# One list of steps for the late stages of a hybrid residual block: gates and latent projection with tokens stationary, merge turned by transposes

## The chip, the cores and the metric

The kernel runs on one core of one Trainium2 chip. The time is the device time of one execution in microseconds (us). TensorE (PE in the profile) multiplies, VectorE (DVE), ScalarE (ACT) and GpSimd (POOL) work element by element, and SyncE (SP) only issues DMAs. Each engine takes its own instructions in order; between engines, semaphores say when a tile is ready or free. TensorE multiplies a stationary tile of 128 x 128, loaded first, with a moving tile of up to 512 columns; N is the number of moving columns. Products add up in banks of the accumulator memory of 128 x 512 numbers, of which the kernel has eight, four called `acc` and four called `aux`.

## What is computed

The input has 512 tokens of 2048 channels. One normalised copy `h` feeds three branches, a gate for each, and one output projection:

```python
h = rms_norm(x, norm_g[l])
proj = h @ w_in[l]
(c_gate, b_gate, u, conv_z, c_q, c_kv, k_rope_raw, mla_z,
 mem_q, mem_z, g_conv, g_mla, g_mem) = jnp.split(proj, split_at, axis=-1)
conv_y = b_gate * causal_depthwise_conv(c_gate * u, conv_w[l])
o_conv = (conv_y * jax.nn.silu(conv_z)) @ w_conv_out[l]
...
o_mla = (mla_y * jax.nn.silu(mla_z)) @ w_mla_out[l]
...
o_mem = (mem_y * jax.nn.silu(mem_z)) @ w_mem_out[l]
merged = (jax.nn.sigmoid(g_conv) * o_conv + jax.nn.sigmoid(g_mla) * o_mla
          + jax.nn.sigmoid(g_mem) * o_mem)
x = x + merged @ w_o[l]
```

`mla_y` is latent attention with 16 heads over the 512 tokens, `mem_y` is attention of 4 heads of width 256 into 256 memory tokens. `g_conv`, `g_mla`, `g_mem`, `o_*` and `merged` are 512 x 2048; `w_mla_out` and `w_o` are 2048 x 2048, `w_mem_out` and `w_conv_out` 1024 x 2048.

## The kernel before

**Products.** Every matrix is kept as two parts, hi and lo, whose sum is the number in fp32. `split` (L121) makes them: ACT copies to hi (L122), DVE subtracts to lo (L124); `weights` (L137) does the same for a weight chunk (L146, L147). One product of two such matrices is three matmuls, `mm3` (L150): hi by hi (L153), hi by lo (L154), lo by hi (L155). A weight chunk is one DMA of 512 KB, 128 partitions x 1024 numbers.

**Two layouts.** A dense product can have the weights stationary and the tokens moving (mode "F", the result has channels on the partitions), or the tokens stationary and the weights moving (mode "T", the result has tokens on the partitions). Both move N = 512 columns.

**Seven products for eight.** The large late projections are cut into 2 x 2 blocks of channels and tokens and use seven block products, P1 to P7, in place of eight. Sums of blocks of the weights are made by DVE as they come (L893 in `s_weights`, L1028 in `t_run`), sums of blocks of the tokens once ahead (`form_sums` L834, in `Forms.build` and `build_forms`). `s_group` (L906) keeps the weights stationary: a block of tokens is then 256 wide, so its matmuls move N = 256, and 512 output columns take 336 of them. `t_run` (L997) keeps the tokens stationary: the weights move with N = 512, and 1024 output columns take 336 matmuls. Before, only `w_o` uses `t_run`.

**Stages.** The memory's keys and values, the latents, the 16 heads, then two groups of memory queries (`mem_queries` L737) with two heads of memory attention each (`mem_attend` L752), then the late stages:

1. `memz`: a dense product in mode "F" over 16 chunks in two groups (L1095 to L1113); its result, through SiLU, multiplies the memory attention's output, which has gone through memory (`mydram`). Meanwhile DVE and ACT make the block sums of `h` (`build_forms`, `place_t1`).
2. 24 `s_group`s in one `s_run` (L966): eight for the convolution branch, four for `mla_z`, twelve for the gates (four each for `g_mem`, `g_conv`, `g_mla`), whose sigmoid is stored to memory (`gdram`) with channels on the partitions.
3. `mem_out`: `branch` (L1172), a dense product in mode "F"; each result times its gate goes to `mdram`. Beside it the block sums for the next stage are made.
4. `mla_out`: four `s_group`s; each result times its gate, plus `mdram`, goes back to `mdram`.
5. `conv_out`: `branch` again; the result times its gate plus `mdram` is the merged row, with channels on the partitions as `w_o` needs it, and `conv_result` makes its block sums.
6. `w_o`: two groups of `t_run`, plus x, to the output.

**Order.** Each stage opens pools of buffers of its own and closes them at its end; a buffer of the next stage lies where one of the last lay, and its first writer waits for the last reader there. The compiler's scheduler sets the order on all engines but SP, whose queue keeps the order of the program. That one queue carries the weight chunks and, between them, the loads of `araw`, `e`, `o`, `sg`, `gm`, `m` and `x` (activations, gates, partial merges, input). `t_run` loads weights eight chunks ahead; `s_group` loads its eight chunks at its first step; `branch` loads its activations at its first four steps.

Of the kernel before, what the change touches and what calls it, by code (L numbers as in the profile page):

```python
# [43 lines left out]
BUILD = (0, 2, 3, 5, 6, 8, 9, 12)  # L44
# [50 lines left out]
def body(ctx, tc, a, out):  # L95
# [11 lines left out]
    wpool = Lines(ctx.enter_context(tc.tile_pool(name="wts", bufs=2)), small, "wts")  # L107
    small.tile([P, SMALL_FILL], F32, name="fill")
    top = ctx.enter_context(tc.tile_pool(name="top", bufs=1, side="right"))
    top.tile([P, TOP_FILL], F32, name="topfill")  # L110
    dram = ctx.enter_context(tc.tile_pool(name="dram", bufs=1, space=bass.MemoryType.DRAM))
# [693 lines left out]
    for _ in mem_query_steps(1, banks_m):  # L805
# [6 lines left out]

    adram = dram.tile([32, P, S], F32, name="adram")
    gdram = dram.tile([48, P, S], F32, name="gdram")
    mdram = dram.tile([KB, P, S], F32, name="mdram")
    PRODUCTS = (("P1", "X", "00"), ("P7", "Y", "T3"), ("P5", "Z", "T1"), ("P6", "W", "T2"),
                ("P2", "X", "10"), ("P4", "Y", "T4"), ("P3", "Z", "11"))

    def tokens_of(b0, b1, f):

        return {"00": (b0[:, 0, :HS], b0[:, 1, :HS]), "T1": (b0[:, 0, HS:], b0[:, 1, HS:]),  # L830
                "10": (b1[:, 0, :HS], b1[:, 1, :HS]), "11": (b1[:, 0, HS:], b1[:, 1, HS:]),
                "T3": (f[:, 0, 0], f[:, 1, 0]), "T2": (f[:, 0, 1], f[:, 1, 1]), "T4": (f[:, 0, 2], f[:, 1, 2])}

    def form_sums(e, o, t, t1):  # L834
        vec.tensor_tensor(out=t[:, 0], in0=o[:, HS:], in1=e[:, HS:], op=ALU.subtract)
        vec.tensor_tensor(out=t[:, 1], in0=t[:, 0], in1=e[:, :HS], op=ALU.add)
        vec.tensor_tensor(out=t[:, 2], in0=o[:, :HS], in1=t[:, 1], op=ALU.subtract)
        vec.tensor_tensor(out=t1, in0=e[:, HS:], in1=e[:, :HS], op=ALU.subtract)

    class Forms:  # L840


        def __init__(self, name):
            self.p, self.close = open_pool(name, "right")
            mk = lambda n, w: [self.p.tile([P, 2] + w, F32R, name=f"{n}{p}") for p in range(8)]
            self.b0, self.f, self.b1 = mk("b0", [S]), mk("f", [3, HS]), mk("b1", [S])
            self.B = [tokens_of(*t) for t in zip(self.b0, self.b1, self.f)]

        def build(self, p, e, o, pool_, first=False):

            b0, b1, f = self.b0[p], self.b1[p], self.f[p]
            t = pool_.tile([P, 3, HS], F32, tag="t", name="t", bufs=2)
            form_sums(e, o, t, e[:, HS:])
            split(e, b0[:, 0], b0[:, 1])
            split(t, f[:, 0], f[:, 1])
            split(o, b1[:, 0], b1[:, 1])

    def open_weights():

        nonlocal psw, close_sw  # L860
        psw, close_sw = open_pool("swts", "left")
        psw.tile([P, KC, 512], F32, tag="raw", name="raw", bufs=6)
        sraw[0] = sform[0] = 0

    psw = close_sw = None
    sraw, sform, sbank = [0], [0], [0]

    def load_s(src):
        i = sraw[0]
        sraw[0] = (i + 1) % 10  # L870
        p = wpool if i % 5 < 2 else psw
        t = p.tile([P, KC, 512], F32, tag="raw", name="raw", bufs=4 if p is wpool else 6)
        t = t.rearrange("p k n -> p (k n)")
        nc.sync.dma_start(t, src)
        return t

    def s_weights(name, w, ch):

        w00, w01, w11, w10 = (w[2 * i + ch] for i in range(4))
        if name == "P1":  # L880
            src = w00
        elif name == "P2":
            src = w10
        elif name == "P4":
            src = w11
        elif name == "P7":
            src = psw.tile([P, KC, 512], F32, tag="s3", name="s3", bufs=2).rearrange("p k n -> p (k n)")
            vec.tensor_tensor(out=src, in0=w00, in1=w01, op=ALU.subtract)
        else:
            src = w01  # L890
            i0, i1, op = {"P5": (w01, w11, ALU.add), "P6": (w01, w00, ALU.subtract),
                          "P3": (w10, w01, ALU.subtract)}[name]
            vec.tensor_tensor(out=src, in0=i0, in1=i1, op=op)  # L893
        i = sform[0]
        sform[0] = (i + 1) % 3
        p = wpool if i < 2 else psw
        hi = p.tile([P, KC, 512], F32R, tag="whi", name="whi", bufs=2 if p is wpool else 1)
        lo = p.tile([P, KC, 512], F32R, tag="wlo", name="wlo", bufs=2 if p is wpool else 1)
        hi, lo = (t.rearrange("p k n -> p (k n)") for t in (hi, lo))
        split(src, hi, lo)  # L900
        return tuple(t.rearrange("p (k n) -> p k n", k=4) for t in (hi, lo))

    def pair(t):
        return t.rearrange("p (b t) -> p b t", b=2)

    def s_group(src, consume, B, pr, add=None):  # L906

        sbank[0] += 1  # L910
        tag = "acc" if sbank[0] % 2 else "aux"
        w, bk, sc = [], {}, {}
# [39 lines left out]
        for name, bn, xn in PRODUCTS:  # L952
            def products(ws, name=name, bn=bn, xn=xn):
                first = bn not in bk
                if first:
                    bk[bn] = bank(tag)
# [459 lines left out]
```

## Time and profile before

| | |
|---|---|
| time, median of 3 runs | 2211.53 us (2210.7 to 2213.6) |
| the profiled execution | 2212.02 us |
| its span, first to last instruction | 2209.8 us, mean granted TensorE clock 0.994 |
| busy: PE, DVE, ACT, POOL | 2151.9, 1604.6, 1026.5, 159.5 us |
| memory moved by DMA | 317.87 MB |
| memory attention, second half, with `memz` | 614 to 721 us |
| 24 `s_group`s | 721 to 1689 us |
| `mem_out` | 1693 to 1782 us |
| `mla_out` | 1782 to 1947 us |
| `conv_out` | 1954 to 2042 us |
| `w_o` | 2044 to 2205 us |

The stages run one after the other on TensorE, so the difference of two starts is a stage's time. The spans and waits below are read from the one profiled execution. In a row of a timeline the columns are the start, the duration, the engine, the line, the operation, what it writes and reads, how many such rows are taken together, and in brackets the idle time just before with what ended it. In a table of windows they are the window, its length, then for PE, weight loads, DVE, ACT and POOL the busy time and number of instructions, then the granted clock, the share of the DMA engines and GB/s.

### The profile page before, as it was taken

To read this page: it belongs to the slowest core of one execution; us is meant where nothing else is said; L and a number is where in the kernel's file an instruction comes from. 1 tells how busy PE (TensorE), PEld (TensorE's weight loads), DVE (VectorE), ACT (ScalarE), POOL (GpSimd) and SP (SyncE) were. 2 spreads that over 40 slices of the span, in tenths; PEclk is the share of its full clock that TensorE was granted. 3 is DMA by queue.
4 is the path that set the end of the run, shared out by engine and by line. 5 is a ranking of instruction groups with operands and counts; after the bars stand their busy time and mean duration, and the time that the engine had idled before them with its cause. 6 is when DMAs were issued, how large, how long until landed. Compare 5 with 4: busy or idle time off the path is not lost.

```text
span 2209.8 us, 35712 instructions
## 1 busy us (share of the span) xinstructions
PE 2151.9 (97%) x14456; PEld 1991.8 (90%) x14456; DVE 1604.6 (73%) x2195; ACT 1026.5 (46%) x1547; POOL 159.5 (7%) x147
## 2 busy tenths in 40 slices
PE   7999999999999999999999999999999999989999
PEld 5788889888887999999999999999998899978787
DVE  7853777774448887887887777767766778867887
ACT  5532677764334444444444444444444434433443
POOL 7510311120000000000000000000000000000000
PEclk9999999999999999999999999999999999999999
DMA  7573212244234433323444344343334755366463
GB/s 260 161 254 105 81 63 68 67 148 148 86 100 160 152 114 119 106 91 130 139 151 164 125 134 141 122 150 115 115 134 151 260 199 189 136 207 231 162 200 115
DMA packets 109845, 317.87 MB, mean 144 GB/s; under 512 B 12144, under 2 KB 12400, under 8 KB 109680
## 3 DMA queue, kind: packets, MB, share of 16 engines
q1 hardware_dynamic: 85296, 269.10, 37.1%
q10 hardware_dynamic: 22784, 41.25, 5.0%
q0 software_dynamic: 1600, 5.24, 0.7%
q8 instruction: 113, 1.85, 0.3%
q14 instruction: 52, 0.43, 0.1%
HBM read 267.31 MB, written 48.23 MB: 143 GB/s over the span
## 4 chain that ended last, share of the span: by engine, by line
PE 89%; DVE 4%; ACT 2%; issue 1%; DMA 1%; POOL 1%; SPq 0%; ACTq 0%; DVEq 0%; POOLq 0%
PE acc L153 16%; PE acc L154 16%; PE acc L155 16%; PE aux L154 12%; PE aux L153 12%; PE aux L155 12%; DVE wlo L147 1%; PE aux L204 1%; PE aux L660 1%; DVE wlo L124 1%; ACT whi L146 1%; POOL xs L304 1%; DVE hT L126 0%; PE aux L640 0%; PE aux L641 0%
## 5 line engine op out<-in xcount | busy, mean ns | idle before, releaser
L122 ACT ACTIVATE whi<-raw 128x1024 fp32r<-128x1024 f32 x392 | 415.3, 1060 | 626.3 <-PE acc L154 236.1
L124 DVE TENSOR_TENSOR wlo<-raw,whi 128x1024 fp32r<-128x1024 f32 x392 | 477.6, 1222 | 162.3 <-ACT whi L122 161.9
L147 DVE TENSOR_TENSOR wlo<-raw,whi 128x1024 fp32r<-128x1024 f32 (+3 forms) x153 | 187.6, 1227 | 173.0 <-ACT whi L146 170.7
L146 ACT ACTIVATE whi<-raw 128x1024 fp32r<-128x1024 f32 (+3 forms) x153 | 152.0, 993 | 218.1 <-PE acc L155 78.5
L893 DVE TENSOR_TENSOR raw<-raw 128x1024 f32<-128x1024 f32 x168 | 205.4, 1223 | 25.6 <-DMA raw<-in_w_conv 7.6
L153 PE MATMUL acc<-f,whi 128*128 128x256 f32 x672 | 190.3, 283 | 1.6 <-ACT whi L122 1.6
L155 PE MATMUL acc<-f,wlo 128*128 128x256 f32 x672 | 190.3, 283 | 0.8 <-DVE wlo L124 0.8
L153 PE MATMUL aux<-f,whi 128*128 128x256 f32 x672 | 190.2, 283 | 0.0
L154 PE MATMUL aux<-f,whi 128*128 128x256 f32 x672 | 190.2, 283 | 0.0
L155 PE MATMUL aux<-f,wlo 128*128 128x256 f32 x672 | 190.2, 283 | 0.0
L154 PE MATMUL acc<-f,whi 128*128 128x256 f32 x672 | 190.2, 283 | 0.0
L153 PE MATMUL acc<-blk,whi 128*128 128x256 f32 (+1 forms) x448 | 134.4, 300 | 2.9 <-ACT z L1110 2.2
L153 PE MATMUL acc<-hU,whi 128*128 128x256 f32 (+1 forms) x448 | 133.8, 299 | 0.0
L154 PE MATMUL acc<-blk,whi 128*128 128x256 f32 (+1 forms) x448 | 133.7, 299 | 0.0
L154 PE MATMUL acc<-hU,whi 128*128 128x256 f32 (+1 forms) x448 | 133.6, 298 | 0.0
L155 PE MATMUL acc<-blk,wlo 128*128 128x256 f32 (+1 forms) x448 | 132.4, 299 | 0.4 <-DVE wlo L147 0.4
L155 PE MATMUL acc<-hU,wlo 128*128 128x256 f32 (+1 forms) x448 | 131.7, 298 | 0.0
L153 PEld LDWEIGHTS acc<-f,whi 128*128 128x128 f32 x672 | 129.0, 192 | 1.8 <-ACT whi L122 1.8
L155 PEld LDWEIGHTS acc<-f,wlo 128*128 128x128 f32 x672 | 129.0, 192 | 1.0 <-DVE wlo L124 1.0
L153 PEld LDWEIGHTS aux<-f,whi 128*128 128x128 f32 x672 | 129.0, 192 | 0.0
L154 PEld LDWEIGHTS aux<-f,whi 128*128 128x128 f32 x672 | 129.0, 192 | 0.0
L155 PEld LDWEIGHTS aux<-f,wlo 128*128 128x128 f32 x672 | 129.0, 192 | 0.0
(399 smaller groups left out, 6055.3 us busy)
## 6 DMA issues: line engine op xcount, KB each, us to landing
raw<-in_w_conv SPq DMA_DIRECT2D x64, 512.0 KB, 4.1
raw<-in_w_o SPq DMA_DIRECT2D x40, 512.0 KB, 4.8
raw<-in_w_mlaz SPq DMA_DIRECT2D x32, 512.0 KB, 3.6
raw<-in_w_gmem SPq DMA_DIRECT2D x32, 512.0 KB, 3.6
raw<-in_w_gconv SPq DMA_DIRECT2D x32, 512.0 KB, 3.7
raw<-in_w_gmla SPq DMA_DIRECT2D x32, 512.0 KB, 3.6
raw<-in_w_mla_out SPq DMA_DIRECT2D x32, 512.0 KB, 4.5
raw<-in_w_mem_kv SPq DMA_DIRECT2D x31, 512.0 KB, 3.6
```

The costliest lines, as they stand in the source:

```text
L122: act.activation(hi, src, AF.Copy, scale=1.0 if g is None else g)
L124: vec.tensor_tensor(out=lo, in0=src, in1=r32(hi), op=ALU.subtract)
L146: act.activation(hi[:, cols], raw[:, cols], AF.Copy)
L147: vec.tensor_tensor(out=lo[:, cols], in0=raw[:, cols], in1=r32(hi[:, cols]), op=ALU.subtract)
L153: nc.tensor.matmul(o, lhsT=s[0], rhs=m[0], start=start, stop=False, skip_group_check=shared)
L154: nc.tensor.matmul(o, lhsT=s[0], rhs=m[1], start=False, stop=False, skip_group_check=shared)
L155: nc.tensor.matmul(o, lhsT=s[1], rhs=m[0], start=False, stop=stop, skip_group_check=shared)
L204: nc.tensor.transpose(out=b[:, i * P:(i + 1) * P], in_=s, identity=ident)
L304: pool.tensor_tensor(out=xs, in0=xraws[k // KC][:, k % KC], in1=scale, op=ALU.mult)
L660: nc.tensor.transpose(out=b[:, i * P:(i + 1) * P], in_=ps[i][:, j * P:(j + 1) * P], identity=ident)
L893: vec.tensor_tensor(out=src, in0=i0, in1=i1, op=op)
```

## The change

The late stages, from `memz` to `w_o`, are written anew as one list of steps with one set of buffers.

- **Buffers.** One pool `work` is opened after the pools of weights, memory keys and values and memory queries are closed. It has 35 tiles of 128 x 1024: six for hi and lo parts of weights (`wf`), ten (`w`) for raw weight chunks and, at times, activations, and nineteen (`q`) for everything else.
- **Steps.** A step has `forms` (fetch a chunk, make a block sum, split it), `products` (its matmuls) and things to do `after`. The forms of a step are written after the products of the step before, across the ends of stages too. Weights are fetched up to eight chunks ahead, over the ends of stages, on SP's queue, which now carries nothing else from `memz` on. Activations, gates, partial merges and x are loaded on POOL's queue, at steps named in the program.
- **Groups.** `f_group` is the former `s_group` in steps of one chunk (24 matmuls of N = 256); the convolution branch and `mla_z` use it. `t_group` is the former `t_run` (steps of 12 matmuls of N = 512, 1024 output columns in 28 steps); the gates (six groups), `mla_out` (two) and `w_o` (two) use it. It reads 20 chunks for 1024 columns where two `s_group`s read 16. The first group of `mla_out` and of `w_o` takes its products in another order (`LEAD_ORDER`), chunks 0 to 2 of P1, P7, P5 and P6 first, and reads 24 chunks. `d_group` is the dense product: `memz` in mode "F" as before, `mem_out` and `conv_out` now in mode "T".
- **Layout.** Gates, `mdram` and the merged rows have tokens on the partitions. `mla_out`'s results are added to `mdram` by POOL's DMA (`accum_op`), not read back and added by DVE.
- **Turning the merge.** `w_o` needs the merged rows with channels on the partitions. `turn` makes them: 16 transposes by TensorE and four copies by ACT after each of the four groups of `conv_out`, then the block sums.

The core of the diff:

```diff
-    open_weights()
-    pz, close_z = open_pool("memz", "left")
...
-    sgroups = [s_group(a["w_conv"][cb], conv_group(cb), BX, pr) for cb in range(8)]
-    sgroups += [s_group(a["w_mlaz"][grp], mlaz_group(grp), BX, pr) for grp in range(4)]
-    for n, nm in enumerate(("w_gmem", "w_gconv", "w_gmla")):
-        sgroups += [s_group(a[nm][grp], gate_group(16 * n + 4 * grp), BX, pr) for grp in range(4)]
-    s_run(sgroups)
...
+    close_w()
+    NQ, NW, NF = 19, 10, 6
+    work, close_work = open_pool("work", "left")
...
+    def fetch(key):
+        k = place[key]
+        while issued[0] < len(loads) and (issued[0] <= k or (issued[0] < k + AHEAD and wlive[0] < cap[0])):
+            kk, src = loads[issued[0]]
+            issued[0] += 1
+            raws[kk] = w("raw")
+            nc.sync.dma_start(flat(raws[kk]), src)
+        return raws[key]
...
+    T_ORDER = [(n, c) for names in (("P1", "P7"), ("P5", "P4"), ("P6",), ("P2",), ("P3",))
+               for c in range(4) for n in names]
+    LEAD_ORDER = [(n, c) for cs in ((0, 1, 2), (3,)) for n in ("P1", "P7", "P5", "P6") for c in cs] + \
+                 [(n, c) for n in ("P4", "P2", "P3") for c in range(4)]
...
+    for b, nm in enumerate(("w_gmem", "w_gconv", "w_gmla")):
+        for grp in range(2):
+            t_group(a[nm][grp], BX, gate_group(b, grp))
...
+        def store(t, n, r):
+            nc.gpsimd.dma_start(at(mdram, t, n), r, accum_op=ALU.add)
...
+    for grp in range(2):
+        t_group(a["w_mla_out"][grp], BA, mla_group(grp), lead=grp == 0)
...
+    def turn(grp):
+        E, O = q("E"), q("O")
+        for f in range(4):
+            b = transpose4([ready[grp, i // 2][:, i % 2, f * P:(f + 1) * P] for i in range(4)],
+                           "aux" if grp % 2 else "acc")
+            act.activation((O if f % 2 else E)[:, f // 2], b, AF.Copy)
+        build(BO, grp, E, O)
...
+    for grp in range(2):
+        t_group(a["w_o"][grp], BO, out_group(grp), lead=grp == 0)
+    for grp in range(4):
+        steps[first + 4 * grp + (4 if grp < 3 else 5)].after.append(lambda grp=grp: turn(grp))
+    ws = steps[0].forms()
+    for i, st in enumerate(steps):
+        st.products(ws)
+        if i + 1 < len(steps):
+            ws = steps[i + 1].forms()
+        for f in st.after:
+            f()
```

The order of instructions moves in three places that the prediction speaks of. The first is ACT in the second half of the memory attention (`mem_attend`; `qh` and `ph` are hi parts of its queries and probabilities, `p` the exponentials, `my` its output, `whi` the hi part of a `memz` weight chunk). Before:

```order
L122 ACTIVATE qh_6794<-aux,gains 128x512
L122 ACTIVATE qh_6803<-aux,gains 128x512
L146 ACTIVATE whi<-raw 128x1024 x2
L778 ACTIVATE p,sm<-aux,nm 128x256 x4
L146 ACTIVATE whi<-raw 128x1024
L122 ACTIVATE ph_6862<-aux 128x512
L122 ACTIVATE ph_6871<-aux 128x512
```

With the change, up to the first `memz` weights:

```order
L121 ACTIVATE ph_6968<-aux 128x512
L121 ACTIVATE ph_6977<-aux 128x512
L799 ACTIVATE my<-aux 128x512 x2
L800 DMA mydram<-my 128x512 x2
L121 ACTIVATE whi<-raw 128x1024
L121 ACTIVATE f<-t 128x512
```

Before, splits of `memz` weights stand between the attention's own steps; now the first of them stands behind the last output of the second head. The order of TensorE's matmuls moves with it.

The second place is SP's queue from `mla_out` to `conv_out` (`gm` are gates and partial merges, `araw` raw activations, `raw` weight chunks). Before:

```order
L1240 DMA gm_20886<-gdram_7004 128x2x512
L1240 DMA gm_20889<-mdram_7005 128x2x512
L1180 DMA araw_20933<-adram_7003 128x512
L1180 DMA araw_20935<-adram_7003 128x512
L134 DMA raw_20943<-in_w_conv_out 128x1024
L1180 DMA araw_20973<-adram_7003 128x512
```

With the change:

```order
L850 DMA raw_17732<-in_w_mla_out 128x1024
L850 DMA raw_17751<-in_w_mla_out 128x1024
L850 DMA raw_17770<-in_w_conv_out 128x1024
L850 DMA raw_17789<-in_w_conv_out 128x1024
L850 DMA raw_17941<-in_w_conv_out 128x1024
```

The first chunk of the next stage no longer stands behind the last gates of the stage before and the activations' loads.

The third place is DVE where `conv_out` ends and `w_o` begins (`sg`, `m`, `g` are gates and merged rows, `t`, `b0`, `b1` block sums of the tokens, `raw` and `wlo` weights). Before:

```order
L1257 TENSOR_TENSOR sg_21632<-acc_21482,sg_21632 128x512
L835 TENSOR_TENSOR t_21615<-m_21611,m_21605 128x256
L124 TENSOR_TENSOR b16_20921<-m_21611,b16_20921 128x512
L1258 TENSOR_TENSOR m_21634<-m_21634,sg_21632 128x512
L836 TENSOR_TENSOR t_21615<-t_21615,m_21605 128x256
L838 TENSOR_TENSOR m_21605<-m_21605 128x256
L835 TENSOR_TENSOR t_21638<-m_21634,m_21628 128x256
L837 TENSOR_TENSOR t_21615<-m_21611,t_21615 128x256
L124 TENSOR_TENSOR wlo_21675<-raw_21658,whi_21674 128x1024
```

With the change:

```order
L123 TENSOR_TENSOR wlo_18703<-raw_18662,whi_18702 128x1024
L1297 TENSOR_TENSOR g_18600<-aux_18487,g_18600 128x512
L962 TENSOR_TENSOR raw_18662<-raw_18662,raw_18692 128x1024
L1297 TENSOR_TENSOR g_18600<-aux_18488,g_18600 128x512
L962 TENSOR_TENSOR raw_18690<-raw_18690,raw_18696 128x1024
L1297 TENSOR_TENSOR g_18604<-aux_18489,g_18604 128x512
L1358 TENSOR_TENSOR m_18602<-m_18602,g_18600 128x1024
L1297 TENSOR_TENSOR g_18604<-aux_18490,g_18604 128x512
L962 TENSOR_TENSOR raw_18692<-raw_18692,raw_18698 128x1024
L123 TENSOR_TENSOR wlo_18721<-raw_18688,whi_18720 128x1024
```

Before, the first `w_o` weights are split behind the merge and the block sums; now weight sums and splits of `w_o` (L962, L123) stand between the last multiplications by the gate.

789 lines of the change are left out of this document (414 added, 375 removed).

## The prediction

> **What bounds the kernel now.** I read the page first: busy times and the chain of waits.
>
> ```profile
> span 2209.8 us, 35712 instructions
> PE 2151.9 (97%) x14456; PEld 1991.8 (90%) x14456; DVE 1604.6 (73%) x2195; ACT 1026.5 (46%) x1547; POOL 159.5 (7%) x147
> PE 89%; DVE 4%; ACT 2%; issue 1%; DMA 1%; POOL 1%; SPq 0%; ACTq 0%; DVEq 0%; POOLq 0%
> ```
>
> TensorE is busy 97% of the span and is 89% of the chain; DVE, at 73%, is the only other engine that could matter. So a change gains by less TensorE time per product, or by filling TensorE's gaps. The second view is the table of windows over the late stages:
>
> ```profile
> 614.00:669.00 55.00, 55.00 (x282) 46.55 (x281) 26.05 (x48) 20.00 (x42) 2.54 (x4) 1.00 0.29 89
> 669.00:721.00 52.00, 48.77 (x211) 38.76 (x210) 45.39 (x75) 22.29 (x31) 4.63 (x9) 1.00 0.52 183
> 1205.00:1688.00 483.00, 483.00 (x4028) 483.00 (x4027) 347.74 (x320) 220.07 (x251) 0.00 (x0) 1.00 0.38 124
> 1688.00:1693.00 5.00, 1.00 (x10) 0.80 (x8) 2.02 (x4) 3.25 (x6) 0.00 (x0) 0.82 0.59 197
> 1693.00:1782.00 89.00, 89.00 (x382) 73.47 (x383) 61.23 (x94) 35.64 (x46) 0.00 (x0) 0.97 0.76 266
> 1787.00:1941.00 154.00, 151.61 (x1260) 151.15 (x1260) 124.42 (x115) 62.99 (x66) 0.00 (x0) 1.00 0.46 157
> 1941.00:1954.00 13.00, 6.13 (x51) 5.93 (x50) 7.89 (x9) 2.32 (x3) 0.00 (x0) 0.87 0.71 251
> 1954.00:2042.00 88.00, 88.00 (x382) 72.68 (x383) 60.24 (x92) 31.41 (x39) 0.00 (x0) 0.98 0.66 229
> 2042.00:2060.00 18.00, 12.96 (x44) 9.29 (x43) 17.93 (x27) 9.29 (x11) 0.00 (x0) 0.81 0.52 189
> 2130.00:2204.00 74.00, 74.00 (x328) 61.10 (x327) 58.55 (x54) 28.65 (x30) 0.00 (x0) 1.00 0.41 130
> 2204.00:2210.00 6.00, 1.15 (x6) 0.61 (x4) 1.38 (x2) 0.00 (x0) 0.00 (x0) 1.00 0.23 87
> ```
>
> Inside the `s_group`s (1205 to 1688) TensorE never rests; the gaps lie at the ends of stages, where the granted clock drops too (.82, .87, .81). A busy TensorE is not one at its peak, so the third view is the timeline, for the pace at both widths, each by its first and last row:
>
> ```profile
> 1499.83 0.28 PE L153 MATMUL aux<-blk,whi 128*128 128x256 f32 x1
> ...
> 1504.51 0.28 PE L153 MATMUL aux<-f,whi 128*128 128x256 f32 x1
> ```
>
> 39 starts apart: 4.68/39 = .120 us for one matmul of N = 256.
>
> ```profile
> 2149.79 0.39 PE L154 MATMUL aux<-wlo,f 128*128 128x512 f32 x1
> ...
> 2158.18 0.39 PE L154 MATMUL aux<-wlo,b 128*128 128x512 f32 x1
> ```
>
> 37 starts apart: 8.39/37 = .2268 us for one of N = 512, in `w_o`, which already keeps the tokens stationary.
>
> **Term 1, the wider matmul.** The gates are twelve groups of 336 matmuls with N = 256: 4032 × .120 = 483.8 us. With tokens stationary they are six groups of 336 with N = 512: 2016 × .2268 = 457.2. That is −26.6. `mla_out` goes from 1344 × .120 = 161.3 to 672 × .2268 = 152.4: −8.9. Together −35.5 us, as the same numbers pass in .2268 in place of .240.
>
> The Trainium skill ("TensorE: Matmul & The Clock Gate", section "Back-to-back issue gap") speaks against so large a gain: it gives the isolated gap of a matmul as N/2.4 + 2.5 ns, so that 512 columns cost 215.8 ns as one matmul and 218.3 as two, and term 1 would be 2688 × 2.5 ns = 6.7 us, an estimate from that page. It says itself that the formula leaves out the weight loads and is too low for small N. The trace has .120 in place of .109 for N = 256, and it decides.
>
> Does the rest keep up? In the last `w_o` window the very steps that the gates now take run without rest: PE 74.00 of 74, DVE 58.55. The tightest steps make a weight sum and a split on DVE in the time of twelve matmuls, 12 × .2268 = 2.72 us:
>
> ```profile
> L893 DVE TENSOR_TENSOR raw<-raw 128x1024 f32<-128x1024 f32 x168 | 205.4, 1223 | 25.6 <-DMA raw<-in_w_conv 7.6
> L124 DVE TENSOR_TENSOR wlo<-raw,whi 128x1024 fp32r<-128x1024 f32 x392 | 477.6, 1222 | 162.3 <-ACT whi L122 161.9
> raw<-in_w_mla_out SPq DMA_DIRECT2D x32, 512.0 KB, 4.5
> ```
>
> 1.22 + 1.22 = 2.44, so .28 us is spare. The 40 extra weight chunks (eight more in each of three gate pairs, twelve for `mla_out`, four for `w_o`) hide: 20 chunks of 512 KB in a group of 336 × .2268 = 76.2 us are 138 GB/s, where the old `mem_out` window moved 266; a chunk lands in 4.5 us and is asked for eight ahead. If that cover went, each chunk could cost its 4.5 us: 180 at worst, but nothing points there. The accumulating DMA into `mdram` has no row. Below it costs nothing, above the 4.5 us of a loaded queue; I take nothing, since `conv_out` first reads columns that were added a whole group earlier.
>
> **Term 2, the ends of stages.**
>
> ```profile
> 1692.98 0.79 PE L153 MATMUL aux<-act,whi 128*128 128x512 f32 x1 [4.00 <-ACT whi L146]
> 1694.00 0.63 PE L153 MATMUL aux<-act,whi 128*128 128x512 f32 x1
> 1694.43 0.63 PE L154 MATMUL aux<-act,whi 128*128 128x512 f32 x1
> 1953.80 0.80 PE L153 MATMUL aux<-act,whi 128*128 128x512 f32 x1 [6.87 <-ACT whi L146]
> 2044.47 0.73 PE L153 MATMUL acc<-whi,b 128*128 128x512 f32 x2 [1.63 <-ACT whi L122]
> 2048.08 0.79 PE L154 MATMUL acc<-wlo,b 128*128 128x512 f32 x1 [2.88 <-DVE wlo L124]
> ```
>
> The gates end at 1692.98 − 4.00 = 1688.98; the six matmuls after 2204 end `w_o` near 2205.4. At full rate those four stages need 384 × .2268 = 87.1 twice, 161.3 and 152.4: 487.9. They take 516.4, so 28.5 us are waits and what follows them: behind the first wait starts are .43 apart in place of .23. The first products of `mem_out` and `conv_out` wait for weights that stand on SP behind activations and gates; the second fence on the order shows that queue, and that the change puts the weights ahead. Their splits then run under the last products of the stage before, and the activations come on POOL. So −28.5.
>
> What comes back: at the start of `w_o` (third fence on the order) a weight sum, L962 on `raw_18690`, stands in DVE ahead of two multiplications by the gate, of the last merged rows and of the last transposes. Its input needs a buffer that `conv_out` holds nearly to its end, and then a load of 4.5 us; It is for P5, which has six steps of P1 and P7 ahead of it in `LEAD_ORDER` (16.3 us); but the split for the third of these (`wlo_18721`) stands behind it too. The bounds are nothing and the 2.88 + 1.63 of today with their slow clock, 8 us; I take 4. The other ends and the step from group to group, 0 to 4: I take 2. So +6.
>
> **Term 3, turning the merge.** 64 transposes. Eight in a row in the memory attention:
>
> ```profile
> 645.07 1.04 PE L204 MATMUL aux<-ident,qrow 128*128 128x128 f32 x8
> 645.86 0.47 PE L153 MATMUL acc<-hU,whi 128*128 128x512 f32 x1
> ```
>
> .79/8 = .099 us each, 64 × .099 = +6.3 on TensorE. They stand a quarter group or more behind the products that they need, so I give no wait. Ends: 6.3, and twice that at half clock.
>
> **Term 4, cover that goes.** The first fence on the order shows the loss: before, `memz` weights are split, and their products run, between the steps of the memory attention's second half; now the first follows its last output. In the window 614 to 669 TensorE is busy throughout. Uncovered, one head goes through these rows in turn:
>
> ```profile
> 618.75 0.88 DVE L747 TENSOR_SCALAR qrow<-acc,rs_r 128x256 f32<-128x256 f32 x2 [0.88 <-POOL rs_r L197]
> 623.65 1.27 ACT L122 ACTIVATE qh<-aux,gains 128x512 fp32r<-128x512 f32 x2 [7.25 <-PE aux L204]
> 624.37 1.41 DVE L126 SCALAR_TENSOR_TENSOR ql<-aux,gains,qh 128x512 fp32r<-128x512 f32 x2 [4.75 <-ACT qh L122]
> 628.54 1.53 DVE L772 TENSOR_REDUCE mx<-aux 128x2 f32<-128x512 f32 x2
> 630.25 0.48 ACT L778 ACTIVATE p<-aux,nm 128x256 f32<-128x256 f32 x1 [2.90 <-DVE nm L774]
> 632.41 0.62 DVE L783 TENSOR_SCALAR p<-p,ri 128x256 f32<-128x256 f32 x2
> 637.73 1.29 DVE L124 TENSOR_TENSOR pl<-aux,ph 128x512 fp32r<-128x512 f32 x2 [0.74 <-ACT ph L122]
> 644.13 0.60 ACT L800 ACTIVATE my<-aux 128x512 f32<-128x512 f32 x1 [2.06 <-PE aux L155]
> ```
>
> Squares, power and `qrow`: 3 us, once. Per head: eight transposes .8; `qh` to the end of `ql` 2.1 (624.37 + 1.41 − 623.65); 24 score products × .120 = 2.9; half of `mx` .8, its scaling .3, four exponentials 4 × .48 = 1.9, the last scaling .6; transposes .8; `ph` and `pl` 1.8; 12 products × .23 = 2.8. That is 14.8; the second head's transposes and `q` splits (2.9) fit under the first's last products. With `my` and one weight split (1.06) behind: 3 + 14.8 + 11.9 less about 1 that overlaps = 29. Then `memz`, 87.1: 116 from 614.6, where the old stretch to the first `s_group` (721.2) took 106.6. So +9. Its 14.4 us of TensorE work leave 14 or 15 of idle time. Bounds: 0 if products slip in after all; +20 if that TensorE work runs at half clock and the ramp of 1694 (.2 × 20) comes behind.
>
> The Trainium skill (the same page, section "Part 1: The HAM clock gate") says that an idle window of about 3.4 us puts TensorE back to half its clock, and as long a busy one frees it. By that rule the gaps here, some 3 to 4 us each, could cost half-rate stretches, up to +7 on top as an estimate. The trace agrees so far: half rate after 4.00 us of idle, none in 1787 to 1941 after its shorter waits.
>
> **The sum.** −26.6 − 8.9 − 28.5 + 6 + 6.3 + 9 = −42.7. From the profiled execution's 2212.0 that gives 2169.3; the median of the runs is .5 lower, so **2169 us**.
>
> **Rivals.** *The ends stay* (2189): the wait moves from the activations to DVE, which in `conv_out` makes gates, merges and block sums (60 of 88 us already) with `w_o`'s sums between them. For it speaks the blocked weight sum; against it that weights and activations now come a stage ahead. Price: 20 of the 28.5 come back.
>
> *Nothing waits* (2154): `w_o` starts seamlessly and `memz` still covers the attention: 15 less. For it: those six steps. Against it: the order.
>
> *Slower: DVE sets the pace of the token-stationary steps* (2223). The place is the 16 tightest steps (P7, P5, P6, P3) of each of eight new groups, 128 in all. It decides once a sum and a split take over 2.72 us, and the gain is used up at 42.7/128 = .33 us more, 1.53 us for each. With 1.57 (.42 over a step, from a DVE slowed by the added POOL and DMA traffic) it is 128 × .42 = +54. Against it: `w_o` runs these steps at 74.00 of 74, with loads beside.
>
> *The wide matmul is no cheaper there* (2205): the gates cost .240 for two halves whatever is stationary, and term 1 is nothing. Against it: the two pairs of rows.
>
> By the skill's isolated gap, the time would be 2169 + 35.5 − 6.7 = 2198, an estimate; I give it no chance of its own beyond the last rival's.
>
> **How the numbers follow.** The forecast has .62, with 2155 to 2186 as its own range (attention 0 to 20, ends 0 to 12, transposes). The ends stay .15, nothing waits .10, DVE sets the pace .07, no cheaper .03; .03 is left for a mixture near no change. The range 2152 to 2196 holds most of the first three, about 8 in 10. A change under 0.2% (2207.1 to 2215.9) can't be told from none. Faster: .62 + .15 + .10 + .03 = .90; same .03; slower .07.
>
> **What would show it.** Gate groups starting 76.2 us apart, with DVE near 60 of each; `mem_out` beginning within a microsecond of the last gate product; 14 to 15 us of TensorE idle between 614 and 645 and the first convolution group at about 730; `w_o` some 155 us long with a wait of some microseconds early on. Gate steps over 2.72 us, idle time ahead of `mem_out` or `conv_out`, or an attention over 40 us long would make the prediction wrong.

## The result, and the profile after

The changed kernel takes 2174.1 us, median of four runs (2173.34 to 2174.72), beside 2211.36 for the kernel before; the ratio is 0.983 (95% interval 0.9813 to 0.9847). The forecast was 2169, its own range 2155 to 2186. The profiled execution took 2173.34 us. Its page begins:

```profile
span 2171.5 us, 30437 instructions
PE 2120.9 (98%) x11832; PEld 1857.2 (86%) x11832; DVE 1586.1 (73%) x2101; ACT 1024.2 (47%) x1509; POOL 213.1 (10%) x211
```

TensorE has 2624 matmuls fewer (2688 fewer by the width, 64 transposes more) and 31 us less busy time. The table of windows by stage (columns as before: length, busy time and number of instructions of PE, weight loads, DVE, ACT, POOL, then granted clock, DMA share, GB/s):

```profile
614.00:619.00 5.00, 3.24 (x17) 2.18 (x15) 3.89 (x11) 2.20 (x11) 2.50 (x4) 1.00 0.33 108
619.00:624.00 5.00, 4.28 (x22) 4.06 (x22) 1.76 (x3) 1.21 (x2) 0.00 (x0) 0.66 0.00 0
624.00:629.00 5.00, 2.44 (x14) 1.63 (x13) 3.09 (x11) 2.78 (x10) 0.00 (x0) 0.82 0.01 3
629.00:634.00 5.00, 5.00 (x14) 3.98 (x15) 1.13 (x2) 0.70 (x2) 0.00 (x0) 0.50 0.00 0
634.00:639.00 5.00, 4.35 (x31) 3.74 (x30) 2.07 (x3) 2.06 (x4) 0.00 (x0) 1.00 0.27 105
639.00:644.00 5.00, 2.36 (x12) 1.13 (x12) 3.40 (x12) 3.02 (x10) 0.74 (x1) 1.00 0.00 0
644.00:649.00 5.00, 2.82 (x12) 2.07 (x12) 4.62 (x8) 2.46 (x4) 0.75 (x2) 1.00 0.88 259
...
1222.00:1678.00 456.00, 456.00 (x2013) 377.58 (x2012) 353.59 (x319) 220.57 (x227) 7.94 (x11) 1.00 0.51 171
...
1916.00:2012.00 96.00, 95.16 (x444) 79.15 (x444) 65.36 (x74) 37.14 (x47) 9.95 (x13) 1.00 0.66 215
```

The gates (1222 to 1678) run without a pause with DVE at 353.59 of 456, and from the gates to the end of `w_o` no window of 5 us is below clock 1.00, where the kernel before had .82, .87 and .81 at the ends of stages. The new hole is at 614 to 649: TensorE is busy 24.48 of 35 us there, at clocks down to .50. The timeline of TensorE in the changed kernel, at the starts of the stages and at the waits named:

```profile
615.55 0.39 PE L154 MATMUL acc<-whi,hU 128*128 128x512 f32 x1
648.73 0.50 PE L152 MATMUL acc<-blk,whi 128*128 128x512 f32 x1 [2.18 <-ACT whi L121]
735.90 0.28 PE L152 MATMUL acc<-blk,whi 128*128 128x256 f32 x1
740.97 0.39 PE L154 MATMUL acc<-f,wlo 128*128 128x256 f32 x1 [1.55 <-DVE wlo L123]
1221.55 0.40 PE L152 MATMUL acc<-whi,blk 128*128 128x512 f32 x1
1678.54 0.39 PE L152 MATMUL acc<-whi,acth 128*128 128x512 f32 x1
1765.58 0.39 PE L152 MATMUL acc<-whi,b 128*128 128x512 f32 x1
1915.83 0.39 PE L152 MATMUL acc<-whi,acth 128*128 128x512 f32 x1
1930.20 0.50 PE L153 MATMUL acc<-wlo,acth 128*128 128x512 f32 x1 [0.84 <-DVE wlo L123]
2011.62 0.39 PE L152 MATMUL acc<-whi,b 128*128 128x512 f32 x1
2022.24 0.50 PE L152 MATMUL aux<-whi,f 128*128 128x512 f32 x1 [0.53 <-ACT E L1366]
2166.47 0.39 PE L154 MATMUL aux<-whi,b 128*128 128x512 f32 x1
```

and in the kernel before:

```profile
614.18 0.40 PE L155 MATMUL acc<-whi,hU 128*128 128x512 f32 x1
...
721.16 0.28 PE L153 MATMUL acc<-blk,whi 128*128 128x256 f32 x1
...
2204.76 0.39 PE L155 MATMUL aux<-whi,b 128*128 128x512 f32 x1
```

From here on the *late stretch* is the time from the first convolution product to the start of the last product of `w_o`. Here it is 2166.47 − 735.90 = 1430.6 us; before it was 2204.76 − 721.16 = 1483.6. So the late stages gave 53.0 us, and the first convolution product came 14.7 later (735.90 − 721.16): 38.3 in the span. The stretch leaves out the run-in (all that comes ahead), which differs by a few us from execution to execution, and tells one stage's change better than the whole time. The 14.7 hold some of it: the last product of the memory queries starts at 614.18 before and at 615.55 with the change. From there to the first convolution product, called the *memory stretch* below, it is 107.0 us before and 120.4 with the change, so the memory stage itself takes 13.4 us more.

### The profile page after: what moved, and what is told of

The parts are those of the page before. It is cut to its first block, busy times and chain, and to the rows that moved or that the text cites. A ratio compares the mean times of both kernels' runs of the same rounds, so it can differ in the third digit from the quotient of the medians.

```text
span 2171.5 us, 30437 instructions
## 1 busy us (share of the span) xinstructions
PE 2120.9 (98%) x11832; PEld 1857.2 (86%) x11832; DVE 1586.1 (73%) x2101; ACT 1024.2 (47%) x1509; POOL 213.1 (10%) x211
## 4 chain that ended last, share of the span: by engine, by line
PE 68%; DVE 1%; issue 1%; DMA 1%; ACT 1%; POOL 0%; ACTq 0%; DVEq 0%; POOLq 0%
PE aux L152 12%; PE aux L154 12%; PE aux L153 12%; PE acc L153 10%; PE acc L154 10%; PE acc L152 10%; DMA araw<-adram 1%; DVE wlo L123 0%; PE aux L203 0%; ACT p L777 0%; PE acc L203 0%; ACT whi L121 0%; DVE qrow L746 0%; POOL mdram L1338 0%; DVE r L1232 0%
## 5 line engine op out<-in xcount | busy, mean ns | idle before, releaser
L123 DVE TENSOR_TENSOR wlo<-raw,whi 128x1024 fp32r<-128x1024 f32 x472 | 575.4, 1223 | 277.8 <-ACT whi L121 277.1
L962 DVE TENSOR_TENSOR raw<-raw 128x1024 f32<-128x1024 f32 x160 | 195.6, 1223 | 8.6 <-DMA raw<-in_w_mla_out 2.7
L154 PE MATMUL acc<-whi,blk 128*128 128x512 f32 (+1 forms) x384 | 144.4, 377 | 0.0
L153 PE MATMUL acc<-wlo,blk 128*128 128x512 f32 (+1 forms) x384 | 144.2, 376 | 0.0
L152 PE MATMUL acc<-whi,blk 128*128 128x512 f32 (+1 forms) x384 | 142.1, 384 | 2.1 <-DVE qt L584 1.4
L153 PE MATMUL aux<-wlo,f 128*128 128x512 f32 x320 | 124.5, 389 | 0.0
L154 PE MATMUL aux<-whi,f 128*128 128x512 f32 x320 | 124.5, 389 | 0.0
L152 PE MATMUL aux<-whi,f 128*128 128x512 f32 x320 | 113.2, 389 | 0.5 <-ACT E L1366 0.5
L908 DVE TENSOR_TENSOR raw<-raw 128x1024 f32<-128x1024 f32 x72 | 87.1, 1222 | 1.4
L152 PEld LDWEIGHTS acc<-whi,blk 128*128 128x128 f32 x384 | 72.4, 189 | 14.2 <-ACT kn L562 2.2
L154 PE MATMUL acc<-f,wlo 128*128 128x256 f32 x288 | 81.6, 283 | 1.6 <-DVE wlo L123 1.6
L153 PE MATMUL acc<-f,whi 128*128 128x256 f32 x288 | 81.5, 283 | 0.0
L152 PE MATMUL aux<-f,whi 128*128 128x256 f32 x288 | 81.5, 283 | 0.0
L153 PE MATMUL aux<-f,whi 128*128 128x256 f32 x288 | 81.5, 283 | 0.0
L154 PE MATMUL aux<-f,wlo 128*128 128x256 f32 x288 | 81.5, 283 | 0.0
L152 PE MATMUL acc<-f,whi 128*128 128x256 f32 x288 | 81.5, 283 | 0.0
L154 PEld LDWEIGHTS acc<-whi,blk 128*128 128x128 f32 x384 | 72.5, 189 | 10.2
```

Of the source, the lines that this page charges most:

```text
L123: vec.tensor_tensor(out=lo, in0=src, in1=r32(hi), op=ALU.subtract)
L152: nc.tensor.matmul(o, lhsT=s[0], rhs=m[0], start=start, stop=False, skip_group_check=shared)
L153: nc.tensor.matmul(o, lhsT=s[0], rhs=m[1], start=False, stop=False, skip_group_check=shared)
L154: nc.tensor.matmul(o, lhsT=s[1], rhs=m[0], start=False, stop=stop, skip_group_check=shared)
L908: vec.tensor_tensor(out=src_, in0=fetch(i0), in1=fetch(i1), op=op)
L962: vec.tensor_tensor(out=src_, in0=src_, in1=fetch((gid, other, c)), op=op)
```

## The experiments

Each is the changed kernel with one edit, but for one run of the changed kernel itself and three that have a second edit beside that of an earlier run: the late loads on SP, and the last two.

**The cover of the memory attention.** The buffers that carry the memory stage's weights stay open, and the first eight `memz` chunks use only them:

```diff
-    close_w()
...
+            return wpool.tile([P, KC, 512], F32, tag="raw", name="raw", bufs=4)
...
+        if nf[0] <= FIRST or nf[0] % 3:
+            hi = wpool.tile([P, KC, 512], F32R, tag="whi", name="whi")
+            lo = wpool.tile([P, KC, 512], F32R, tag="wlo", name="wlo")
```

The total of buffers is the same (four raw and four parts here, six raw, two parts and nineteen others in the new pool).

> The changed kernel, but the buffers of the memory stage's weights stay open and carry the first memz weights, so that memz products can stand between the steps of the second half of the memory attention again, as before. My theory (the cover that went costs the whole stretch): the first convolution group, at 735.9 us in the changed kernel and 721.2 before, comes back to 721 to 725, TensorE shows no idle time between 614 and 649, and the time falls by 11 to 15 us, to 2159 to 2163. Rival (the attention's chain of DVE and ACT steps sets that stretch, so products between its steps delay it): the group starts later than 730 and the time falls by less than 6. Rival (the lost time is the clock, not the cover): the waits go but half-clock spacings stay, a fall of about 8.

Measured: 2162.32 us against 2213.64, ratio 0.976 (0.9744 to 0.9777). The windows and the first convolution product of this kernel:

```profile
614.00:649.00 35.00, 35.00 (x179) 29.48 (x178) 16.37 (x32) 14.42 (x33) 2.78 (x4) 1.00 0.20 69
```

```profile
720.41 0.28 PE L152 MATMUL acc<-blk,whi 128*128 128x256 f32 x1
...
2156.78 0.39 PE L154 MATMUL aux<-whi,b 128*128 128x512 f32 x1
```

TensorE does not rest in 614 to 649, the clock stays at 1.00, and the convolution starts at 720.4, 15.5 us sooner. The memory stretch is 104.3 us (104.2 in the two other runs with the cover; 120.0 to 123.1 in the nine without it), 16.1 less than with the change and 2.7 less than before. So the whole loss of the memory stage came from the cover, through the buffers that `memz` has to wait for: SP asks for the first `memz` chunk at 594.1 before, at 615.7 with the change and at 596.1 here. The rivals fall. But the late stretch is 1436.4, 5.8 longer than in the changed kernel, so the whole gains about 11.

**The gates with weights stationary.**

```diff
-        for grp in range(2):
-            t_group(a[nm][grp], BX, gate_group(b, grp))
+        for grp in range(4):
+            f_group(a[nm][grp], BX, gate_rows(b, grp))
```

> The changed kernel, but the twelve gate groups keep the weights stationary again (336 products of N = 256 for 512 columns). It leaves out the gates' layout: they are stored with channels on the partitions, and the merge, which reads them as token rows, multiplies by the wrong gates. My theory (the wider product saves 2016 x (2 x .120 - .2268) = 26.6 us): 2200 to 2202, groups 40.3 us apart. The Trainium skill's isolated gap (2.5 ns for each pair) makes it 2016 x 2.5 ns = 5 us, an estimate: 2179. If it was not the width but the steps of one chunk, the time stays within 2 us of 2174.

Measured: 2203.01 us, ratio 0.9949 (0.9934 to 0.9964). Its gates in one window:

```profile
1221.00:1705.00 484.00, 484.00 (x4035) 484.00 (x4035) 352.92 (x326) 223.62 (x232) 7.58 (x11) 1.00 0.41 137
```

Neither form rests: 484 us of matmuls with N = 256 against 456 to 457 with N = 512. The late stretch is 1458.1, +27.5 for a forecast of 26.6. That the steps of one chunk made the gain, and not the width, is out: it is the width. The 5 us from the Trainium skill's isolated gap ("TensorE: Matmul & The Clock Gate", section "Back-to-back issue gap") are out as well.

**The queue of the loads.** Five of the loads move from POOL to SP:

```diff
-            nc.gpsimd.dma_start(raw[c], two(adram, n0 + 2 * c))
+            nc.sync.dma_start(raw[c], two(adram, n0 + 2 * c))
...
-                    nc.gpsimd.dma_start(tiles[k, t], at(d, t))
+                    nc.sync.dma_start(tiles[k, t], at(d, t))
```

> The changed kernel, but activations, gates, partial merges and x are loaded on SP's queue, between the weights, at the same steps of the program. My theory of the ends of stages (before, the first weights of a stage stood behind activations and gates in one queue): the waits come back in part, 5 to 28 us, 2179 to 2202, most of it ahead of mem_out, conv_out and w_o. Rival (what cured the ends is that everything is asked for six to eight steps ahead into buffers of its own; the queue does not matter): within 3 us of 2174.

Measured: 2171.42 us, ratio 0.9808 (0.9794 to 0.9823), late stretch 1430.5 against 1430.6. My theory of the queue, as I had put it, falls: sharing SP's queue costs nothing by itself. The trace of the kernel before shows what happened there. SP and ACT at the start of `conv_out`, before:

```profile
1944.92 0.94 SPq L1180 DMA_DIRECT2D araw<-adram  x2
1945.91 0.95 SPq L134 DMA_DIRECT2D raw<-in_w_conv_out  x1
```

```profile
1950.80 0.63 ACT L122 ACTIVATE act<-araw 128x512 fp32r<-128x512 f32 x1 [11.53 <-DMA araw<-adram]
```

Activations and weights were asked for from 1944.9 on, behind the last loads of the stage before, some 2 us before TensorE ran out of work; landing and splitting took until 1953.8. At the start of `mem_out` it is another thing:

```profile
1674.33 0.80 SPq L1180 DMA_DIRECT2D araw<-adram  x2
```

```profile
1689.75 1.15 ACT L1156 ACTIVATE r<-r 128x512 f32<-128x512 f32 x2 [4.60 <-DVE r L949]
1690.80 0.61 ACT L122 ACTIVATE act<-araw 128x512 fp32r<-128x512 f32 x1
```

Here the activations were asked for at 1674.3 and the first weights at 1675.2, over 13 us before the last gate product ended at 1689.0, and loads of these two kinds took 2.6 to 3.2 and 4.1 to 6.3 us to land around there. They had landed, but ACT split them only at 1690.8, behind the sigmoids of the last gates (L1156), for whose results it had waited 4.60 us. So the theory of the queue fails at `mem_out` in the old trace already. The next runs ask whether it counts how far ahead of their use activations are loaded and split.

**Asked for late.** The activations of `mem_out` and `conv_out` are loaded and split one step ahead of their use, once on SP and once on POOL:

```diff
-            steps[first - 6 + c].after.append(lambda c=c: load(c))
-            steps[first - 4 + c].after.append(lambda c=c: cut(c))
+            hooks.append((first - 1 + c, lambda c=c: load(c)))
+            hooks.append((first - 1 + c, lambda c=c: cut(c)))
```

> As the run with loads on SP, but the activations of mem_out and conv_out are asked for one step ahead of their use in the program, not six, and split there, as the kernel before did. With the loads on SP but early, the stretch from the first convolution group to the end was the changed kernel's to 0.1 us, so the queue alone costs nothing. Theory now (it is the time of asking: 4.3 us for a load and 1.3 us for each split come between asking and the first product, and before they were asked for behind loads that waited for the stage's last results): waits ahead of mem_out and conv_out come back, 2 to 7 us each, 4 to 14 in all. Rival (the waits before came from each stage's newly opened buffers, which had to be given up by the last stage, and one step is enough where buffers are free): within 2 us of the changed kernel.

> As the run with late loads, but the loads stay on POOL's queue as in the changed kernel: asked for one step ahead of their use in the program, not six. If it is only the time of asking, this is as long as the run with late loads on SP, 2188 to 2193 (+15 to +19). If the queue matters once the loads are late (POOL's queue is free and runs ahead of the program, SP's waits for weight buffers in front of them), most of it goes: 2173 to 2180.

Measured: 2190.98 us on SP (ratio 0.9898, 0.9883 to 0.9913) and 2192.57 on POOL (0.9903, 0.9888 to 0.9918). The late stretches are 1449.7 and 1448.8, +18 to +19. TensorE's waits on SP, then on POOL:

```profile
1680.92 0.61 PE L152 MATMUL acc<-whi,acth 128*128 128x512 f32 x1 [2.82 <-ACT acth L121]
...
1944.12 0.80 PE L152 MATMUL acc<-whi,acth 128*128 128x512 f32 x1 [2.17 <-ACT acth L121]
```

```profile
1679.62 0.80 PE L152 MATMUL acc<-whi,acth 128*128 128x512 f32 x1 [3.37 <-ACT acth L121]
1688.69 0.50 PE L152 MATMUL acc<-whi,acth 128*128 128x512 f32 x1 [1.87 <-ACT acth L121]
...
1931.29 0.79 PE L152 MATMUL acc<-whi,acth 128*128 128x512 f32 x1 [5.71 <-ACT acth L121]
```

The same waits come back on either queue, at the places where the kernel before had its 4.00 and 6.87, and without buffers newly opened by a stage (these kernels have none). So it counts that a stage's activations are loaded and split well ahead, and not which queue loads them. But the edit moves the load and the split together, and the traces tell them apart. The run with late loads on POOL, at `mem_out`:

```profile
1606.29 0.72 POOL L1267 DMA_DIRECT2D araw<-adram  x1 [424.88 <-PE aux L154]
```

```profile
1677.03 1.04 ACT L1246 ACTIVATE r<-r 128x1024 f32<-128x1024 f32 x1
1678.52 1.06 ACT L121 ACTIVATE acth<-araw 128x1024 fp32r<-128x1024 f32 x1 [0.44 <-ACT r L1246]
```

POOL ran so far ahead of the program that the first activations were asked for 73 us before their product, and TensorE still waited 3.37 us: the split stood behind a gate's sigmoid (L1246) in ACT's order. At `conv_out` it was the load:

```profile
1919.55 0.90 POOL L1267 DMA_DIRECT2D araw<-adram  x1
```

```profile
1930.19 1.06 ACT L121 ACTIVATE acth<-araw 128x1024 fp32r<-128x1024 f32 x1 [3.74 <-DMA araw<-adram]
```

It took over 10 us to land. On SP it is the same: no split of `mem_out` waited for its load, two at `conv_out` did, 3.47 and 5.63 us. So my theory of the time of asking holds at `conv_out`; at `mem_out` it is the place of the split. No run moves one without the other.

Of the 28.5 us that went at the ends, nearly two thirds come back with this one edit. TensorE's waits for activations are 8.7 us on SP and 11.0 on POOL, within the 4 to 14 that I gave; I left out what follows a wait. In each run the clock is at half for 13.6 us around these waits, which costs some 5 to 7 us more; a few short waits for weights are the rest.

**The lead order.**

```diff
-        t_group(a["w_mla_out"][grp], BA, mla_group(grp), lead=grp == 0)
+        t_group(a["w_mla_out"][grp], BA, mla_group(grp), lead=False)
...
-        t_group(a["w_o"][grp], BO, out_group(grp), lead=grp == 0)
+        t_group(a["w_o"][grp], BO, out_group(grp), lead=False)
```

> The changed kernel, but the first groups of mla_out and w_o take the same order of products as the others (fourth chunk in steps 7 and 8, 16 us in, where the lead order has it in steps 13 to 16), and read 20 chunks, not 24. My theory (w_o has to wait for the last merged rows, their transposes and block sums, which are ready some 14 to 18 us into the group): 1 to 8 us longer at the start of w_o, nothing at mla_out, 2175 to 2182. Rival (the block sums are ready in time, and the lead order only costs loads and sums): 2172 to 2174.

Measured: 2183.64 us, ratio 0.9868 (0.9854 to 0.9883), late stretch 1442.4, +11.8. The two longest waits of TensorE in it, and between them the two for block sums (`b`):

```profile
1853.26 0.50 PE L153 MATMUL acc<-wlo,b 128*128 128x512 f32 x1 [1.63 <-DVE wlo L123]
...
2036.32 0.74 PE L152 MATMUL acc<-whi,b 128*128 128x512 f32 x2 [0.26 <-ACT b L121]
...
2040.75 0.50 PE L154 MATMUL acc<-whi,b 128*128 128x512 f32 x1 [0.98 <-DVE b L123]
...
2108.06 0.50 PE L153 MATMUL aux<-wlo,f 128*128 128x512 f32 x1 [2.58 <-DVE wlo L123]
```

The lead order is worth more than I thought, and partly for another reason. `w_o` gets 7.3 us longer, as my theory said, but only 1.2 of it are waits for the block sums, .26 and .98, some 16 and 20 us into its first group. `mla_out` also gets some 4 longer, which the theory did not say, and the two longest waits are for weight splits 6 to 8 us into each second group; half clock from 2108.9 to 2112.3 follows the last. The lead order also spreads DVE's work: it puts P6's sums in the first half of a group, so that they do not stand just ahead of P3's. That this is the reason for the rest is not shown; no run separates it from the four extra loads.

**The changed kernel again**, as the base of the next runs.

> The changed kernel itself once more, on the chip of this group of runs, as their base: 2171 to 2177.

Measured: 2173.57 us, ratio 0.9822 (0.9806 to 0.9837), late stretch 1431.8.

**The transposes twice.**

```diff
-        for i, s in enumerate(src):
+        for i, s in [x for _ in range(times) for x in enumerate(src)]:
```

> The changed kernel with each of the 64 transposes of the merged rows done twice into the same bank. My theory (they stand on TensorE's own time at .099 us each and nothing waits): +6.3 us, conv_out and the start of w_o longer by that. Rival (the transposes run in gaps that are there anyway): within 1 us. Rival (they come late and w_o waits for what they make): over 10.

Measured: 2179.61 us, ratio 0.985 (0.9836 to 0.9865); +6.0 on the run before it, late stretch 1437.4, +5.6 on that run and +6.8 on the first profile. That is the 6.3 of 64 × .099: they stand on TensorE's own time and nobody waits.

**More work for DVE.** In the gates, a step with a weight sum makes its lo part twice:

```diff
+            if other and extra:
+                vec.tensor_tensor(out=flat(r[1]), in0=flat(src_), in1=r32(flat(r[0])), op=ALU.subtract)
```

> The changed kernel; in the gate groups each step with a weight sum makes its lo part twice on DVE (1.22 us more, same result), 3.66 us in a step of 2.72. By the price that my slower rival was given (each such step waits for DVE): 96 x .94 = +90 us, 2264. By averages (P7 and P5 steps alternate with P1 and P4 steps of 1.22, 2.44 a step on average; only the four P6 and the four P3 steps in a row exceed, 3.8 us for each run of four, less the two steps that the forms can be ahead): 0 to 2.5 us for each of twelve runs, 0 to 30 us in all.

Measured: 2189.77 us, ratio 0.9894 (0.9878 to 0.9911), +16 on the base, late stretch 1445.6. Its gates:

```profile
1222.00:1688.00 466.00, 459.45 (x1997) 372.33 (x1996) 452.17 (x412) 216.34 (x225) 7.24 (x10) 1.00 0.50 165
```

DVE's busy time in the gates rises from 353.59 to 452.17 us, nearly the whole window; the gates get 9 us longer and `mem_out`, with which their last products now mix, 5. The price "each heavy step waits" (+90) is far off, and the forecast by averages (0 to 30) holds. Steps lend each other time: DVE had 456 − 353.59 = 102 us to spare in the changed kernel's gates, and they took up most of the added work (98.6 us more busy time in the window). Not all, though the sum would have fitted: TensorE's longest waits, .8 us each, come once in each of the six groups, where heavy steps stand in a row.

**Two versions of the cover.** Cover with the loads on SP, and cover with the buffers used in another order:

```diff
-        if zlive[0] < NZ:
+        if zlive[0] < NZ and (issued[0] <= FIRST or wlive[0] - zlive[0] >= cap[0] - NZ):
```

> Cover restored and, beside it, the loads on SP's queue. In the run with cover the memory stage gave back 15.5 us and the later stages took 5.2 us more than the changed kernel's, most of it in mla_out, where weights waited for buffers. If POOL's slower loads (8.9 us to landing in mla_out) hold buffers of that stage, this gains 2 to 5 on the run with cover, 2157 to 2160; if the buffers are held by the weights themselves, the same as with cover, 2161 to 2164.

> Cover restored, but after the memz stage's first group a weight chunk takes one of the six buffers of the late stages first and one of the four kept from the memory stage only when those are taken. If the 5.2 us that the run with cover lost in the later stages come from how weights are spread over the two sets of buffers, they change: 2156 to 2160 where it was that, 2161 to 2166 where it was not.

Measured: 2160.44 us (ratio 0.9756, 0.974 to 0.9773) and 2162.09 (0.9766, 0.9751 to 0.9781), against cover alone with 0.976 (0.9744 to 0.9777). The late stretches are 1434.5, 1435.4 and 1436.4. The intervals lie over each other: neither is shown to be better than cover alone, and why the late stages take 4 to 6 us more with the cover is left open. All three beat both kernels: some 11 to 14 us under the change.

## Why the prediction was right, and where it was off

The time lay 5 us above the forecast, inside its own range. By terms, forecast and measured:

| term | forecast | measured |
|---|---|---|
| gates and `mla_out` with N = 512 | −35.5 | gates 1678.54 − 1221.55 = 457.0 (457.2 forecast); without it +27.5 (26.6) |
| ends of stages | −28.5 + 6 | the stages from `mem_out` on take 488.2 where 485.3 is full rate; 1.7 more at the first convolution group |
| turning the merge | +6.3 | doubled, +5.6 to +6.8 |
| cover of the memory attention | +9 | +13.4 in the memory stretch, and 1.4 of run-in, which no term had |
| sum in the profiled execution | −42.7 | −38.7 |

**Term 1 held.** Two rows of the old trace, .120 and .2268, gave the gain to within 1 us, and the run with the gates turned back confirms it. *The wide matmul is no cheaper there* is out. So is the time by the Trainium skill's isolated gap.

**Term 2: size right, cause wrong.** The ends cost what the old windows said (28.1 rather than 28.5, as the last product of `w_o` starts at 2204.76), and nearly all of it went: full rate is now 487.9 − 8.9 + 6.3 = 485.3, and 2.9 us of waits are left, with the 1.7 at the first convolution group 4.6 for the 6 that I gave back. But the step "the first products wait for weights that stand on SP behind activations and gates" failed: with the loads back on SP nothing was lost. At `conv_out` what had cost the time was the late asking, for weights and activations together, behind loads that could only go once results of the stage before were in; at `mem_out` both had landed, and their splits stood on ACT behind the sigmoids of the last gates. The size held all the same, since it came from the old windows and not from this step, and since the change moved the splits ahead too. That much was luck. Of the 28 us some 7 are not waits but what follows them: in the kernel before the clock is at half for 6.8 us at each of three ends, with 13.5 us of TensorE's work in them. The 4 us given for the start of `w_o` was mostly not there: one wait of .53, for the copies of the last transposed rows; the weight sum held nothing up. The 2 for all other ends became waits of .84 and 1.55.

**Term 3 held**, in place and size.

**Term 4: mechanism right, mis-sized.** The memory stretch grew by 13.4 us for the 9 that I gave. `memz` took its 87.2 (648.73 to 735.90, 87.1 forecast), so the 4.4 are in the uncovered chain. Two things were left out of its 29 us. The sum names the last `my` and the first weight split, but 3 + 14.8 + 11.9 − 1 does not hold them; they are 1.7. And the clock, which I had only as the upper end: it was at half in 620.3 to 623.8 and 627.2 to 634.0. The 24 score products of the first head and its 12 products with the values ran at half pace for part of the time: the scores took 4.7 us (619.69 to the last start at 624.29 and .12) for 2.9, the values, with four transposes among them, 5.7 (628.87 to 634.55) for 3.2. The idle time was 10.5 of the 35 us for the 14 or 15 that I expected, so part of this was made up; how much each step weighs in the 4.4 is not separated. Rows of the changed kernel's timeline:

```profile
617.68 0.44 PE L203 MATMUL aux<-ident,qrow 128*128 128x128 f32 x2 [1.30 <-DVE qrow L746]
618.58 0.44 PE L203 MATMUL aux<-ident,qrow 128*128 128x128 f32 x2 [0.46 <-DVE qrow L746]
619.69 0.39 PE L152 MATMUL aux<-mkh,qh 128*128 128x256 f32 x1 [0.67 <-ACT qh L121]
...
620.85 0.41 PE L152 MATMUL aux<-mkh,qh 128*128 128x256 f32 x1
621.06 0.41 PE L153 MATMUL aux<-mkl,qh 128*128 128x256 f32 x1
...
626.39 0.63 PE L203 MATMUL aux<-ident,p 128*128 128x128 f32 x4 [1.83 <-DVE p L782]
```

The score products start .21 apart in place of .12. The sentence on the Trainium skill's clock gate (the same page, section "Part 1: The HAM clock gate") put up to 7 us on top. An idle window of 3.4 us, which it speaks of, is not in these rows as one wait, since none ahead of the half pace was longer than 1.83; but 3.4 us is the length of the first stretch at half clock.

**The rivals.** *Nothing waits* was nearly true for the ends and wrong for the attention. *The ends stay* is out; the late loads show that 18 us would have been its price. *DVE sets the pace* was not only unlikely but wrongly priced: breakeven was set at .33 us for each heavy step, and 1.22 us more on each of 96 cost 16.

## What to carry to other kernels

A matmul's pace at each width, read as spacing from rows of the same trace, forecasts a change of width to a per cent; do it before trusting a formula. At the end of a stage, ask when the next stage's first tiles can be loaded, and also what stands ahead of their splits on the engine that makes them, not which queue loads them: early loads and splits cost nothing on either queue, late ones 18 us on both. And when buffers are re-arranged, look for work that covered a serial chain far from the edit: here a pool opened over the memory attention's buffers took back 13.4 of the 53 us gained, and keeping eight buffers open made the whole 11 us faster.

## What was not expected of the hardware

TensorE's clock fell after several short waits. In the changed kernel 1.30, .46 and .67 us of waiting, 2.4 together within 3.3 us, were followed by half clock from 620.34 to 623.75, and one wait of 1.83 by half clock from 627.16 to 633.99. Like waits later (1.86, .21 and .58 between 639 and 644, and 2.18 before 648.73) were not; the windows from 634 to 649 stand at 1.00.

```profile
620.34:623.75 3.41, 3.36 (x16) 3.28 (x16) 0.84 (x3) 0.00 (x0) 0.00 (x0) 0.50 0.00 0
...
627.16:633.99 6.83, 6.24 (x18) 4.82 (x19) 1.61 (x4) 1.48 (x3) 0.00 (x0) 0.50 0.01 2
...
637.40:640.81 3.41, 1.83 (x14) 1.62 (x14) 1.96 (x6) 1.39 (x7) 0.00 (x0) 1.00 0.00 0
```

The stretches come in one length: 3.4 us or twice that. So it is in all nine runs without the cover, between 610 and 660, and at the ends of stages. In the kernel before, half clock stands at 1691.17 to 1698.00, 1950.58 to 1957.4 and 2046.17 to 2052.99, and from each of these six times to the next it is a whole multiple of 3.413 us (2, 74, 2, 26 and 2), to .1 us. So in these traces the clock changes at ticks some 3.41 us apart, and a fall costs at least 3.4 us at half. In the 3.41 us ahead of each fall inside the memory stage TensorE was busy 1.1 to 2.0 us; but between 637.40 and 640.81 it was busy 1.83 and the clock stayed, so these traces give no sharp limit. The length of one wait does not tell whether the clock falls, and the same stage had its falls at different places from run to run, two in most, three or four in others.
